# RMSNorm with ReLU on one core: one semaphore per SBUF slot that counts its loads and stores, in place of one per transfer

## The chip, the cores and the metric

The kernel runs on one core of a Trainium2 chip. The metric is device time in microseconds (us) of one execution; the times given are medians of several executions. The profile is one further look at a single execution; its span, from the first to the last instruction, is about 1.8 us shorter than the time.

## The reference

```python
# x: 16 x 1024 x 512 float32, gamma: 512 float32, eps = 1e-5
rms = np.sqrt(np.mean(x ** 2, axis=-1, keepdims=True) + eps)
return np.maximum(x / rms * gamma, 0).astype(np.float32)
```

Each of the 16384 rows is read once and written once: 33.55 MB in and 33.55 MB out, 67.11 MB in all.

## The kernel before

The rows are cut into 8 chunks of 4 MB, each 128 partitions by 16 rows of 512 numbers. SBUF has 6 slots of that size. SP issues every load and store; DVE multiplies in place; a chunk's result is stored from the slot that it was loaded into. Chunk 0 is loaded in two halves so that compute may start early. Chunks 6 and 7 use slots 0 and 1 again, and are loaded once stores 0 and 1 have landed. A "block" is half a chunk, 8 rows a partition; there are 16, and the semaphore `done` counts them.

```python
loads = [(0, 0, G), (0, G, K - G)] + [(i, 0, K) for i in range(1, nchunks)]
sem_ld = [tc.alloc_semaphore(f"ld{i}") for i in range(len(loads))]   # 9
sem_st = [tc.alloc_semaphore(f"st{i}") for i in range(nchunks)]      # 8
# ... sem_g, sem_e, sem_z, ready, sq, done, sa, sv

for m, (i, a, r) in enumerate(loads):       # SP
    if i < nslots:
        load(m)
nxt = nslots
for i in range(nchunks):
    nc.sync.wait_ge(done, per * (i + 1))
    store(i)
    if i >= 1 and nxt < nchunks:
        nc.sync.wait_ge(sem_st[nxt - nslots], 16)
        # ... load(m) of chunk nxt
        nxt += 1

for m, (i, a, r) in enumerate(loads):       # POOL tells ACT what has landed
    nc.gpsimd.wait_ge(sem_ld[m], 16)
    nc.gpsimd.sem_inc(ready, r // G)

# ... ACT: 16 blocks of squares, sums and roots; DVE: reciprocal, x * rstd * gamma, relu
#     then_inc(done, 1) on each relu

with nc.sync.register("landed") as landed:  # SP, at the end
    nc.sync.reg_mov(landed, 16)
    for i in range(nchunks):
        nc.sync.wait_ge(sem_st[i], landed)
```

## Time and profile before

| | before |
|---|---|
| time, median of the first 3 runs | 162.71 us (162.61 to 162.89) |
| span of the profiled run | 161.2 us |
| bytes moved, mean rate | 67.12 MB, 416 GB/s over the span |
| DVE, ACT busy | 126.0 us, 86.3 us |
| last landing of a store, end of the span | 160.04 us, 161.16 us |

The costliest groups of compute (line, engine, operation, tiles, shape, count; then busy us, mean ns of one; then idle time before them and what ended it) and the issues of transfers (count, size, median us from issue to landing) of the kernel before:

```profile
L115 ACT ACTIVATE junk<-slots 128x512 f32 x128 | 74.5, 582 | 30.8 <-ACTq L111 30.5
L139 DVE SCALAR_TENSOR_TENSOR slots<-slots,rstd,gamma_sb 128x512 f32 x128 | 86.2, 747 | 4.8 <-DVEq L136 4.8
...
out_dram<-slots SPq DMA_DIRECT2D x8, 4096.0 KB, 31.4
slots<-in_x_dram SPq DMA_DIRECT2D x7, 4096.0 KB, 30.4
```

ACT waits 30.5 us for data. A store takes 31.4 us from issue to landing, yet its 4 MB take only about 9.8 us of the engines at 430 GB/s (4.19 MB by the rate that the stretches of the prediction show): most of the rest it stands in the queue behind others.

### The profile page before, as it was taken

Reading aid. Unit: us, or ns where it says so; the run is one execution under the profiler, and the core shown is the slowest. Engines: PE = TensorE matmul, PEld = TensorE weight load, DVE = VectorE, ACT = ScalarE, POOL = GpSimd, SP = SyncE. Lnnn points to the kernel's source line nnn. Section 1 sums busy time; section 2 is a strip of 40 time slices with the busy share of each in tenths; the row PEclk is TensorE's granted clock in tenths of the full one; section 3 lists DMA queues with packets and bytes.
Section 4 is the critical chain, followed back from the end, with each engine's and each line's share of the span. In section 5 each row is a group of like instructions: output and inputs, shape, how many; then the busy total and the mean of one; then the engine's idle time right before and its main releaser. Section 6 shows DMA issues by size and latency. Waiting matters only on the chain. (4 is left out here: it accounts for less than half of the span.)

```text
span 161.2 us, 1006 instructions
## 1 busy us (share of the span) xinstructions
DVE 126.0 (78%) x164; ACT 86.3 (54%) x273; POOL 0.2 (0%) x4
## 2 busy tenths in 40 slices
DVE  1103989898989898999999999999999999993000
ACT  3088929889988988988900298503994000000000
POOL 0000000000000000000000000000000000000000
DMA  5999999999999999999999999999999999999993
GB/s 155 433 439 431 496 390 415 496 390 399 512 390 390 512 399 390 390 399 512 390 399 504 399 399 496 407 399 488 407 407 488 407 407 480 415 407 464 431 390 138
DMA packets 2456, 67.12 MB, mean 416 GB/s; under 512 B 276, under 2 KB 276, under 8 KB 280
## 3 DMA queue, kind: packets, MB, share of 16 engines
q1 hardware_dynamic: 2448, 67.11, 97.4%
q10 hardware_dynamic: 8, 0.01, 0.0%
HBM read 33.56 MB, written 33.55 MB: 416 GB/s over the span
## 5 line engine op out<-in xcount | busy, mean ns | idle before, releaser
L115 ACT ACTIVATE junk<-slots 128x512 f32 x128 | 74.5, 582 | 30.8 <-ACTq L111 30.5
L139 DVE SCALAR_TENSOR_TENSOR slots<-slots,rstd,gamma_sb 128x512 f32 x128 | 86.2, 747 | 4.8 <-DVEq L136 4.8
L146 DVE TENSOR_SCALAR slots<-slots x16 | 36.7, 2294 | 2.4 <-DVEq L145 0.2
L115 ACT ACTIVATION_READ_ACCUMULATOR junk<-slots x128 | 23.9, 187 | 0.0
L133 DVE RECIPROCAL rstd<-rms x16 | 3.2, 197 | 6.4 <-DVEq L129 6.4
L122 ACT ACTIVATE rms<-ss,eps_sb x16 | 4.8, 301 | 3.0 <-ACTq L121 3.0
L126 DVE LOAD_MASK_SELECT gamma_sb<-gseed x1 | 0.0, 14 | 5.8 <-DMA gseed<-in_gamma_dram 5.8
L107 ACT ACT_TABLE_LOAD x1 | 1.3, 1283 | 2.8 <-issue 2.8
L100 DVE MEMSET gseed<- 128x512 f32 x1 | 0.5, 485 | 1.1 <-SPq L81 1.1
L126 DVE STREAM_SHUFFLE gamma_sb<-gseed 128x512 f32<-128x512 f32 x1 | 0.7, 716 | 0.0
L168 POOL MEMSET const-bfloat16-1.0<- 128x1 bf16 x1 | 0.1, 102 | 0.0
L168 POOL MEMSET const-uint8-127<- 128x1 uint8 x1 | 0.1, 102 | 0.0
L168 POOL MEMSET const-float32-1.0<- 128x1 f32 x1 | 0.1, 99 | 0.0
L168 POOL MEMSET const-float32-0.0<- 128x1 f32 x1 | 0.1, 98 | 0.2 <-issue 0.2
L101 DVE MEMSET eps_sb<- 128x1 f32 x1 | 0.1, 59 | 0.0
## 6 DMA issues: line engine op xcount, KB each, us to landing
out_dram<-slots SPq DMA_DIRECT2D x8, 4096.0 KB, 31.4
slots<-in_x_dram SPq DMA_DIRECT2D x7, 4096.0 KB, 30.4
slots<-in_x_dram SPq DMA_DIRECT2D x2, 2048.0 KB, 9.7
gseed<-in_gamma_dram ACTq DMA_DIRECT2D x1, 8.0 KB
```

Of the source, the lines that this page charges most:

```text
L100: nc.vector.memset(gseed, 0.0).then_inc(sem_z, 1)
L101: nc.vector.memset(eps_sb, eps).then_inc(sem_e, 1)
L107: nc.scalar.preload_act_table(ACTF.Sqrt)
L115: a = nc.scalar.activation(out=junk[:, j, :], in_=slots[:, bass.ds(base + j * d, d)], func=ACTF.Square, accum_out=ss[:, bass.ds(col + j, 1)])
L122: nc.scalar.activation(out=rms[:, bass.ds(col, G)], in_=ss[:, bass.ds(col, G)], func=ACTF.Sqrt, bias=eps_sb, scale=inv_d).then_inc(sq, 1)
L126: nc.vector.stream_shuffle(gamma_sb, gseed, [0] * 32)
L133: nc.vector.reciprocal(out=rstd[:, bass.ds(col, G)], in_=rms[:, bass.ds(col, G)]).then_inc(sv, 1)
L139: r = nc.vector.scalar_tensor_tensor(out=row, in0=row, scalar=rstd[:, bass.ds(col + j, 1)], in1=gamma_sb, op0=ALU.mult, op1=ALU.mult)
L146: nc.vector.tensor_scalar_max(out=blk, in0=blk, scalar1=0.0).then_inc(done, 1)
L168: nc = _bacc.Bacc("TRN2", target_bir_lowering=False, num_devices=1)
```

## The change

The intent is to need fewer semaphores: 6 slot counters and one for the first half-load, where there were 9 and 8, and one for both memsets where there were two. Loads and stores of a slot alternate, so the counter goes up by 16 with each, and the thresholds follow from the turn: 16 loaded, 32 stored, 48 loaded again, 64 stored again.

```diff
@@ -54,10 +54,11 @@
 
 
     loads = [(0, 0, G), (0, G, K - G)] + [(i, 0, K) for i in range(1, nchunks)]
-    sem_ld = [tc.alloc_semaphore(f"ld{i}") for i in range(len(loads))]
-    sem_st = [tc.alloc_semaphore(f"st{i}") for i in range(nchunks)]
+
+
+    sem_half = tc.alloc_semaphore("half")
+    sem_slot = [tc.alloc_semaphore(f"slot{s}") for s in range(nslots)]
     sem_g = tc.alloc_semaphore("gam")
-    sem_e = tc.alloc_semaphore("epsr")
     sem_z = tc.alloc_semaphore("zero")
     ready = tc.alloc_semaphore("ready")
     sq = tc.alloc_semaphore("sq")
@@ -72,10 +73,18 @@
     def load(m):
         i, a, r = loads[m]
         nc.sync.dma_start(out=slot_ap(i)[:, a:a + r, :],
-                          in_=xv[i][:, a:a + r, :]).then_inc(sem_ld[m], 16)
+                          in_=xv[i][:, a:a + r, :]
+                          ).then_inc(sem_half if m == 0 else sem_slot[i % nslots], 16)
+
+    def loaded(engine, m):
+        i = loads[m][0]
+        if m == 0:
+            engine.wait_ge(sem_half, 16)
+        else:
+            engine.wait_ge(sem_slot[i % nslots], 32 * (i // nslots) + 16)
 
     def store(i):
-        nc.sync.dma_start(out=ov[i], in_=slot_ap(i)).then_inc(sem_st[i], 16)
+        nc.sync.dma_start(out=ov[i], in_=slot_ap(i)).then_inc(sem_slot[i % nslots], 16)
 
     ctx.enter_context(tc.manual_schedule(engines={mybir.EngineType.SP}))
     with tc.tile_critical():
@@ -87,25 +96,25 @@
             nc.sync.wait_ge(done, per * (i + 1))
             store(i)
             if i >= 1 and nxt < nchunks:
-                nc.sync.wait_ge(sem_st[nxt - nslots], 16)
+                nc.sync.wait_ge(sem_slot[nxt % nslots], 32)
                 for m, (c, a, r) in enumerate(loads):
                     if c == nxt:
                         load(m)
                 nxt += 1
 
         for m, (i, a, r) in enumerate(loads):
-            nc.gpsimd.wait_ge(sem_ld[m], 16)
+            loaded(nc.gpsimd, m)
             nc.gpsimd.sem_inc(ready, r // G)
 
         nc.vector.memset(gseed, 0.0).then_inc(sem_z, 1)
-        nc.vector.memset(eps_sb, eps).then_inc(sem_e, 1)
+        nc.vector.memset(eps_sb, eps).then_inc(sem_z, 1)
 
         nc.scalar.wait_ge(sem_z, 1)
         nc.scalar.dma_start(out=gseed[0:P:32, :],
                             in_=gamma[None, :].to_broadcast([P // 32, d])
                             ).then_inc(sem_g, 16)
         nc.scalar.preload_act_table(ACTF.Sqrt)
-        nc.scalar.wait_ge(sem_e, 1)
+        nc.scalar.wait_ge(sem_z, 2)
         with nc.scalar.Fori(0, ngroups) as gi:
             nc.scalar.wait_ge(ready, 1)
             nc.scalar.sem_inc(ready, -1)
@@ -146,9 +155,12 @@
             nc.vector.tensor_scalar_max(out=blk, in0=blk, scalar1=0.0).then_inc(done, 1)
 
     with nc.sync.register("landed") as landed:
-        nc.sync.reg_mov(landed, 16)
-        for i in range(nchunks):
-            nc.sync.wait_ge(sem_st[i], landed)
+        nc.sync.reg_mov(landed, 32)
+        for s in range(nchunks - nslots, nslots):
+            nc.sync.wait_ge(sem_slot[s], landed)
+        nc.sync.reg_mov(landed, 64)
+        for s in range(nchunks - nslots):
+            nc.sync.wait_ge(sem_slot[s], landed)
 
 
 # ---- launch: one core; inputs and outputs as the reference has them ----
```

## The prediction

> **What bounds the kernel now.** I read the page of the profile first: the span, the busy shares, the slices and the DMA queues.
>
> ```profile
> span 161.2 us, 1006 instructions
> ...
> DVE 126.0 (78%) x164; ACT 86.3 (54%) x273; POOL 0.2 (0%) x4
> ...
> DMA  5999999999999999999999999999999999999993
> ...
> q1 hardware_dynamic: 2448, 67.11, 97.4%
> ```
>
> The reader is to see that no compute engine is near full, and that one queue, the one that the sync engine (SP) fills with all loads and stores, keeps the 16 DMA engines at nine tenths or more in 38 of 40 slices. Next I cut the span into stretches (columns: stretch, its length, busy time of DVE, ACT and POOL with counts, granted clock, DMA share, GB/s).
>
> ```profile
> 2.00:30.00 28.00, 15.29 (x22) 18.08 (x55) 0.00 (x0) 1.00 1.01 429
> 30.00:60.00 30.00, 28.36 (x38) 27.63 (x90) 0.00 (x0) 1.00 1.00 427
> 60.00:90.00 30.00, 28.21 (x37) 19.32 (x63) 0.00 (x0) 1.00 1.01 429
> 90.00:120.00 30.00, 28.51 (x38) 18.64 (x60) 0.00 (x0) 1.00 1.00 430
> 120.00:146.00 26.00, 24.66 (x31) 2.62 (x9) 0.00 (x0) 1.00 1.00 430
> 146.00:158.00 12.00, 0.49 (x1) 0.00 (x0) 0.00 (x0) 1.00 1.01 437
> 158.00:161.20 3.20, 0.00 (x0) 0.00 (x0) 0.00 (x0) 1.00 0.03 10
> ```
>
> From 2 to 158 us the DMA share never falls below 1.00, at 427 to 437 GB/s. The 67.12 MB of the page at 430 GB/s are 156.1 us, which is this stretch. Compute ends at 146.5 us (start 144.20 plus 2.29, the last row of the timeline) and the transfers run 12 us longer. So the sum that sets the time is: about 1.5 us of start, 156 us of transfers, and a tail of about 3 us with nothing in transfer. Then I asked the waits of the DMA-issuing queue on SP (total us, times, longest us).
>
> ```profile
> SPq L78 <- DVE slots L146: 105.4, 6, 26.6
> SPq L74 <- DMA out_dram<-slots: 32.9, 2, 24.1
> SPq L151 <- DMA out_dram<-slots: 12.5, 2, 9.6
> ```
>
> SP waits 105.4 us for finished blocks and 32.9 us for two slots to come free; all of that lies beneath transfers already queued, as the full DMA share shows. Only the end of the third line (L151, the final waits for all stores) is on the path, since nothing follows the last landing but the end of the program. For that tail I read three source lines: the program's last one between 160.6 and 161.3 us, the final waits, and the register move ahead of them (count, ns least/median/most, first and last start).
>
> ```profile
> L182 POOLq EVENT_SEMAPHORE_RANGE_CLEAR  x1: 201/201/201, 160.7 to 160.7; - x1
> ...
> L151 SPq EVENT_SEMAPHORE  x4: 17/28/28, 147.4 to 160.1; - x4
> ...
> L149 SPq MOVE  x1: 43/43/43, 147.3 to 147.3; - x1
> ```
>
> The records behind them give the order: the last store's 16 increments land from 158.70 to 160.04 us, SP's last final wait is released at 160.06, all engines meet at 160.5, POOL clears the semaphores from 160.66 to 160.86, and a second meeting ends the span at 161.16. So 1.1 us lie between the last landing and the end, and semaphore instructions are all that is in it.
>
> **What the Trainium skill says.** The page DMA: Bandwidth & Descriptors, section "Why a DMA increments its semaphore by 16 and not by 1", says that each engine taking part adds one when its data has landed, and warns that two transfers in flight on one semaphore can let a wait pass early; it asks for one semaphore per in-flight slot. The trace agrees on the count: 16 landings for each load and store. In its section "Anatomy of one DMA" it says that DMA engines wait on no semaphore, the issuing sequencer does, and that the semaphore write is nearly free beside the write receipt. The trace shows the first side: load 6 was issued at 72.07 us, 16 ns after store 0's last increment at 72.06. The page Perfetto Trace Analysis, section "Per-engine timelines", says that a sequencer-only instruction's record holds its execution alone, not its wait or propagation; hence the 17 and 28 ns of the L151 rows are the cost, and the microseconds before them the wait. The page Runtime: NRT & Kernel Launch, section "The ~15µs preamble/postamble breakdown", lists a reset of 51 semaphores per engine around the kernel; [...]no run here shows it. I count nothing for it.
>
> **The change part by part.** I compared both built programs engine by engine: every engine has the same shown instructions in the same order, SP has 40 and POOL 31 in all in both programs, and the transfers are the same with the same shapes. Only which semaphore is named, and against which value, differs.
>
> 1. *Loads and stores.* Same 17 transfers on the same queue; each still adds 16. Which counter it adds to touches no byte that moves. Cost 0.
>
> 2. *The two waits before loads 6 and 7.* Before: store 0's own semaphore at 16. After: slot 0 at 32, which is the second half-load of chunk 0 plus store 0. By the landing records that half-load landed at 13.27 us and store 0 at 72.06, so 32 is reached at 72.06, exactly when the old wait was. For slot 1: load 22.98, store 81.95, so 81.95. On one slot no two transfers fly together on that counter, since each store is issued after its load landed (31.14 after 13.27, 47.62 after 22.98) and each reload after the store; the separate semaphore for the first half keeps even chunk 0 apart. Cost 0.
>
> 3. *POOL's nine waits that tell ACT what has landed.* Still nine, 17 ns each by the trace; they now wait for 16 or 48. 48 on slot 0 is complete when load 6 lands (91.49), as before. Cost 0.
>
> 4. *The two memsets on one counter.* ACT asked for the second memset at 2.79 us, after issuing gamma's transfer; that memset ended at 1.61 (1.551 plus 0.059). A wait for 2 on the shared counter is met just as long before. Cost 0.
>
> 5. *Final waits.* Before: one register move, eight waits packed into four L151 instructions and the closing branch. After: six waits, two register moves. The move to 64 carries slot 2's wait; it costs about 43 ns (the L149 row), but stores 2 to 5 have all landed by 140.62 us and SP gets there at 147.3, so it runs at about 147.5, beneath the last store's transfer. After the last landing, the old program ran a wait on two semaphores (28 ns) and then the branch; the new one runs a wait on slot 1 alone (17 ns, as the single wait in the L151 row) and then the same branch. On the path: minus 11 ns.
>
> 6. *Clearing at the end.* The built programs show it clearing 30 semaphores before and 19 after. It took 201 ns and stands between two meetings of all engines, so it is on the path. If its time is all per semaphore: 201 / 30 = 6.7 ns each, 11 fewer save 74 ns. If it is all fixed: 0. I take half, 37 ns; this is an estimate from one row, and the trace cannot choose.
>
> Sum: 0 - 11 - 37 = -48 ns, bounds about -85 and 0. On the median of 162.71 us that gives 162.66, or -0.03%.
>
> **The rivals.** (a) *The shared counter holds a transfer back.* If a load or the final wait had to wait for something later than before, a gap would open in the DMA share. Against: step 2's times, where the added term landed some 59 us before the deciding one. Even if a reload were issued some microseconds later, store 1 still stood ahead of it in the queue (load 6 was issued at 72.07 us, store 1 landed at 81.95, load 6 at 91.49), so that nothing would idle. The time would stay at 162.7. To cost 2% (3.3 us) the queue would have to run dry, for which nothing speaks. (b) *The shorter counter list saves more than I count.* The whole tail from the last landing to the end is 1.1 us; were a third of it proportional to the number of semaphores, the time would fall by about 0.25 us to 162.45. For it: clearing is the one long instruction there. Against: all else in the tail is meetings of engines, the same in both programs. (c) *The reloaded register falls onto the path.* If the second move ran after the last landing it would add 43 ns, and 162.75 would result; against it, it hangs on slot 2, whose last store lands at 101.46 us. (d) *Another draw of DMA throughput.* The transfers are 97% of the time; 0.2% more or less in their rate is 0.3 us, larger than all my terms, and the three runs of before already spread over 0.28 us (162.61 to 162.89), with a profiled run at 162.94.
>
> **Range and chances.** All rivals of substance stay between 162.45 and 162.75; the spread of runs (d) is wider than they are. I take 162.65 with 162.3 to 163.0: 0.35 us each way, the seen spread of 0.28 and a little for another chip or another hour. For 2% the time has to leave 159.5 to 166.0, and I know of no path that leads there: the lower end would need more than the whole 1.1 us tail to vanish three times over. Chances: faster 0.01, same 0.98, slower 0.01.
>
> **What would show each step right or wrong.** Right: the DMA share at 1.00 from 2 to 158 us and the same reload times (72.1 and 82.0 us, within the run's noise) for steps 1 and 2; nine POOL waits of 17 ns for 3; ACT's first work at 8.8 us for 4; one 17 ns wait after the last landing for 5; a clearing instruction between 127 and 201 ns for 6. The prediction would be wrong if a gap in the DMA share appears before a reload, if a final wait is released well after the last landing, if the clearing grows, or if the rate of the transfers changes with the counter they add to, which I have held to be impossible.

## The result, and the profile after

| | before | after |
|---|---|---|
| time, median of 6 runs each | 162.82 us (162.61 to 162.89) | 162.79 us (162.54 to 163.48) |
| span of the profiled run | 161.2 us | 160.9 us |
| last landing to end of span | 1.112 us | 1.029 us |

The ratio is 1.0005, with a 95% interval of 0.9985 to 1.0025: no difference that can be told. The page of the changed kernel, lines as in the prediction:

```profile
span 160.9 us, 1006 instructions
...
DVE 126.0 (78%) x164; ACT 86.3 (54%) x273; POOL 0.2 (0%) x4
...
DMA  5999999999999998999999999999999999999993
...
q1 hardware_dynamic: 2448, 67.11, 97.6%
```

The instruction counts, the busy times and the bytes are the same. The stretches of the changed kernel (columns as before):

```profile
2.00:30.00 28.00, 15.35 (x22) 18.17 (x55) 0.00 (x0) 1.00 1.01 428
30.00:60.00 30.00, 28.36 (x38) 27.63 (x90) 0.00 (x0) 1.00 1.01 429
60.00:90.00 30.00, 28.21 (x37) 19.23 (x62) 0.00 (x0) 1.00 1.00 427
90.00:120.00 30.00, 28.51 (x38) 18.81 (x60) 0.00 (x0) 1.00 1.00 431
120.00:146.00 26.00, 24.66 (x31) 2.45 (x9) 0.00 (x0) 1.00 0.99 429
146.00:158.00 12.00, 0.43 (x1) 0.00 (x0) 0.00 (x0) 1.00 1.01 437
```

The DMA share stays at 0.99 to 1.01, the rate at 427 to 437 GB/s: no gap opened. A stretch of 30 us would hide a gap of a few tenths of a us, but the packets show none either: between the first data and the last, an engine stood idle for 0.62 us in the mean, as against 0.79 us before. The waits of SP's queue in the changed kernel:

```profile
SPq L87 <- DVE slots L155: 105.2, 6, 26.5
SPq L75 <- DMA out_dram<-slots: 33.0, 2, 24.2
SPq L163 <- DMA out_dram<-slots: 12.4, 1, 12.4
```

The same three waits, within 0.2 us of before. The last is now one wait of 12.4 us in place of two, since the final waits are ordered by slot. By the landing records store 0 lands at 72.114 us and load 6 is issued at 72.131; store 1 at 82.035 and load 7 at 82.051. The last source lines of the changed kernel:

```profile
L194 POOLq EVENT_SEMAPHORE_RANGE_CLEAR  x1: 138/138/138, 160.5 to 160.5; - x1
...
L163 SPq EVENT_SEMAPHORE  x1: 17/17/17, 159.9 to 159.9; - x1
...
L161 SPq MOVE  x1: 29/29/29, 147.4 to 147.4; - x1
```

The clearing of 19 semaphores takes 138 ns, where 30 took 201. The wait released by the last store is a single one of 17 ns, and the second register move is made at 147.4 us, beneath the last store. The tail is 0.083 us shorter. The rest of the 0.25 us between the two spans (160.90 and 161.16 us) is transfers: the last landing came at 159.88 us in this run and at 160.04 in the other.

### The profile page after: what moved, and what is told of

Same layout as the page of the kernel before. It is cut to its first block, busy times and chain, and to the rows that moved or that the text cites. A ratio compares the mean times of both kernels' runs of the same rounds, so it can differ in the third digit from the quotient of the medians.

```text
span 160.9 us, 1006 instructions
## 1 busy us (share of the span) xinstructions
DVE 126.0 (78%) x164; ACT 86.3 (54%) x273; POOL 0.2 (0%) x4
```

## The experiments

My theory: the transfers set the time, no counter holds one of them back, and the only trace of the change is in the tail, by the number of semaphores cleared. Rivals: the shared counters delay a reload; the increments on them cost transfer time; the tail got shorter for another reason. All kernels gave the correct result. Each group of runs has its own runs of the kernel before beside it.

### The size of chance: both kernels once more

No edit: e1 is the kernel before, e2 the changed one, five rounds each.

> The kernel before against itself: the size of chance. My theory (transfers set the time, and their rate wanders by some 0.2%): ratio 1.000 with an interval of about 0.2% each way; the clearing instruction again at 201 ns. A rival that the two semaphore schemes differ by a real few tenths of a per cent would need this interval to be much narrower than the one of the changed kernel.

> The changed kernel once more, with five rounds. My theory: the tail is 0.08 us shorter, the transfers wander by more, ratio 1.000 within 0.2% either way (0.9995 if the tail alone showed); last landing to end of span 1.03 us, clearing 138 ns. Rival (the shared counters slow or delay transfers): ratio of 1.001 or more with an interval that leaves out 1.

| run | median | ratio to before, 95% interval | last landing to end |
|---|---|---|---|
| e1, before against itself | 162.99 us | 1.0007 (0.9994 to 1.0020) | 1.113 us |
| e2, changed kernel | 162.81 us | 0.9993 (0.9980 to 1.0006) | 1.029 us |

The kernel before differs from itself by as much as the changed one differs from it. The rival ratio of 1.001 or more is ruled out by the interval of e2. The tail, however, came out at 1.11 us for the one and 1.03 us for the other both times that each was profiled: a difference of 0.084 us can be read from the trace even though 0.2% of time, 0.3 us, hides it on the clock. The intervals were a little narrower than the 0.2% that I had expected.

### Does the number of semaphores make the tail?

e3 adds 11 semaphores that nothing uses, e4 adds 100:

```diff
     sv = tc.alloc_semaphore("sv")
+    spare = [tc.alloc_semaphore(f"spare{i}") for i in range(11)]   # e4: range(100)
```

> The changed kernel with 11 semaphores allocated and never used, so that 30 are cleared as before, while loads and stores still share the slot counters. My theory (each cleared semaphore costs 5.7 ns, from 201 and 138 ns for 30 and 19): clearing back at 201 ns, last landing to end about 1.09 us, time not told apart from before. Rival (the clearing got shorter for another reason, such as which semaphores stood nonzero or when it started): clearing stays near 138 ns.

> The changed kernel with 100 unused semaphores more, 119 cleared. My theory: clearing takes 29 + 119 x 5.7 = 707 ns, 570 more than in the changed kernel, all on the path: last landing to end about 1.60 us, time about 163.3 us, ratio 1.003. Rival (the cost of clearing is in steps or mostly fixed): clearing under 300 ns, ratio 1.000.

The clearing instruction of e3:

```profile
L195 POOLq EVENT_SEMAPHORE_RANGE_CLEAR  x1: 201/201/201, 160.5 to 160.5; - x1
```

The clearing instruction of e4:

```profile
L195 POOLq DRAIN  x2: 34/131/228, 160.5 to 161.5; - x2
...
L195 POOLq EVENT_SEMAPHORE_RANGE_CLEAR  x1: 680/680/680, 160.8 to 160.8; - x1
```

| semaphores cleared | kernel | clearing | last landing to end | median | ratio to before |
|---|---|---|---|---|---|
| 19 | changed (e2) | 138 ns | 1.029 us | 162.81 us | 0.9993 (0.9980 to 1.0006) |
| 30 | e3 | 201 ns | 1.101 us | 162.78 us | 1.0003 (0.9991 to 1.0014) |
| 30 | before (e1) | 201 ns | 1.113 us | 162.99 us | 1.0007 (0.9994 to 1.0020) |
| 119 | e4 | 680 ns | 1.710 us | 163.43 us | 1.0033 (1.0020 to 1.0046) |

With 30 semaphores the clearing is back at 201 ns to the nanosecond, though the transfers still share their counters: its length goes by the count of semaphores, not by what they count. From 19 to 119 the clearing grows by 542 ns, 5.4 ns each, and the tail by 0.68 us, 6.8 ns each. The tail grows by more than the clearing because the drain on POOL just ahead of it is longer too (88 ns in the changed kernel, 99 ns before and in e3, 228 ns in e4): 542 and 140 ns make the 0.68 us. Why the drain grows is left open. These are means over 11 and 100 semaphores, and a single one need not show: e9 and e10 below clear 20, in 139 ns behind a drain of 83 ns, and their tail is 1.029 us, as with 19. So e4's time was foreseen (163.3 us, measured 163.43), its clearing was 27 ns shorter and its tail 0.11 us longer than foreseen. e3's tail is 12 ns shorter than that of the kernel before with the same 30 semaphores: that is the final wait on one semaphore in place of two, 11 ns by their records.

### What does a met wait cost on the path?

e5 puts the wait for the last store first, so the others come after it.

```diff
+        nc.sync.reg_mov(landed, 64)
+        for s in reversed(range(nchunks - nslots)):
+            nc.sync.wait_ge(sem_slot[s], landed)
         nc.sync.reg_mov(landed, 32)
         for s in range(nchunks - nslots, nslots):
             nc.sync.wait_ge(sem_slot[s], landed)
-        nc.sync.reg_mov(landed, 64)
-        for s in range(nchunks - nslots):
-            nc.sync.wait_ge(sem_slot[s], landed)
```

> The changed kernel with the wait for the last store put first, so that the register move back to 32 and the waits for slots 4, 5, 3 and 2, all met long before, come after the last landing. My theory: a met wait costs 53 to 67 ns from start to start (the spacing of such instructions in the trace), so two instructions more on the path and the move make about 0.13 us: release of the last wait to the closing branch about 0.18 us, in place of 0.057, last landing to end about 1.16 us, the time the same within noise. Rival (waits that are already met cost nothing): tail stays at 1.03 us. Rival (waits against registers are slow): tail longer by 0.5 us or more.

The final waits of e5, from 140 us on:

```profile
L161 SPq MOVE  x1: 29/29/29, 160.1 to 160.1; - x1
...
L163 SPq EVENT_SEMAPHORE  x2: 17/22/27, 160.1 to 160.2; - x2
```

All three now start after the last landing at 160.059 us: at 160.075, 160.139 and 160.192, and the closing branch at 160.260. Here the move carries the wait for the last store. From release to branch are 0.185 us, where the changed kernel has 0.057. The tail is 1.156 us, as foreseen (1.16), and the time is not told apart from before: 162.92 us, ratio 0.9994 (0.9955 to 1.0032; one run of before at 163.87 us widens the interval). A met wait thus costs 53 to 68 ns on the path, far more than the 17 to 28 ns of its record, and register waits are not otherwise slow.

### How much delay could a counter have caused for free?

The prediction held that a reload may come some microseconds later at no cost. Four runs put one more wait before both reloads of the changed kernel, for an event that comes later. In e6 that event is the relu of block 8, in e7 the landing of store 1, in e9 the seventh of eight multiplications of block 8, in e10 the first half of the relu of block 8. It is load 6 that the wait holds back; load 7 is issued at 81.8 to 82.7 us in all four, as against 82.05 in the changed kernel.

```diff
                 nc.sync.wait_ge(sem_slot[nxt % nslots], 32)
+                nc.sync.wait_ge(done, 8)            # e6
+                nc.sync.wait_ge(sem_slot[1], 32)    # e7
+                nc.sync.wait_ge(mid, 8)             # e9, e10: mid is a new semaphore
...
+                if j == G - 2:                      # e9, on the multiplications
+                    r.then_inc(mid, 1)
...
-            nc.vector.tensor_scalar_max(out=blk, in0=blk, scalar1=0.0).then_inc(done, 1)
+            nc.vector.tensor_scalar_max(out=lo, in0=lo, scalar1=0.0).then_inc(mid, 1)   # e10: lo, hi are the halves of blk
+            nc.vector.tensor_scalar_max(out=hi, in0=hi, scalar1=0.0).then_inc(done, 1)  # e10
```

> The changed kernel with both reloads held until eight blocks are done, some 80.6 us, in place of 72.1 us for load 6: the delay that a coarser counter could have caused, 8.5 us. My theory: store 1 keeps the engines busy until about 81.5 us, so nothing idles, the order in the queue is as before, time 162.8, same. Rival (a reload's issue time goes straight into the time): about 8 us longer.

> The changed kernel with load 6 held until store 1, the last transfer in the queue, has landed (82.0 us; 1.5 us later than in the run with eight blocks). My theory: the queue runs dry; from the last data of store 1 (some 81.4 us) to the first data of load 6 (82.05 plus 1.0 us from issue to first data, as at the start of the span) 1.6 to 2.0 us pass with nothing in transfer, and the time grows by that, to 164.4 to 164.8 us, ratio 1.010 to 1.012. Rival (later slack takes the gap up): the same time.

> The changed kernel with both reloads held until DVE has multiplied the seventh of eight rows of block 8, at about 77.5 us: load 6 comes 5.4 us later than in the changed kernel, but still some 3 us before the queue's last data (81.0 to 81.4 us). The run with 80.7 us lost 2.1 us, which my prediction had ruled out. My theory now: a delay is free only while the reload's first data (0.97 us after issue, as that run shows) can come before the engines have drained what is queued, so before an issue at about 79.8 us; here no gap and no slow packets at the reload, time 162.8, ratio 1.000. Rival (a late reload costs in proportion, some 2.1 us for 8.6 us of delay): 1.3 us longer, ratio 1.008.

> As the run before, but held until half of the last relu of block 8, at 79.5 to 80.0 us (the relu is split in two, which lengthens DVE's work by under 0.2 us a block, beneath the transfers): close to the edge. My theory: first data due at 80.5 to 81.0 us, when the first engines drain; no or next to no idle time, and at most a part of the 2.1 us. Rival (proportional): 1.8 us longer, ratio 1.011. If it is as slow as the run at 80.7 us, the edge lies earlier than the first data says[...].

e10 changes two things at once, the relu and the hold. So e11 has the split relu alone:

```diff
-            nc.vector.tensor_scalar_max(out=blk, in0=blk, scalar1=0.0).then_inc(done, 1)
+            nc.vector.tensor_scalar_max(out=lo, in0=lo, scalar1=0.0)
+            nc.vector.tensor_scalar_max(out=hi, in0=hi, scalar1=0.0).then_inc(done, 1)
```

> The control of the run before: the relu split in two as there, but the reloads held by nothing more than in the changed kernel (72.1 us). That run came out 3.0 us longer than before, more than the one held to 80.7 us. If the hold did it: DVE about 1.1 us more busy, reload at some 72.2 us, time 162.8, ratio 1.000. If the split relu did it (later stores, another rhythm of blocks): up to 1.017.

In the table, "packets" is the sum of the recorded times of the data packets, divided by 16 engines, and "idle" what is left of the time from the first data to the last.

| run | load 6 issued | median | ratio to before, 95% interval | packets | idle |
|---|---|---|---|---|---|
| changed kernel | 72.13 us | 162.79 us | 1.0005 (0.9985 to 1.0025) | 156.81 us | 0.62 us |
| e11 (control) | 72.15 us | 163.00 us | 0.9994 (0.9961 to 1.0026) | 156.99 us | 0.72 us |
| e9 | 77.44 us | 162.74 us | 0.9998 (0.9984 to 1.0011) | 156.83 us | 0.63 us |
| e10 | 80.06 us | 165.81 us | 1.0174 (1.0153 to 1.0195) | 158.67 us | 2.28 us |
| e6 | 80.72 us | 164.89 us | 1.0121 (1.0081 to 1.0160) | 158.44 us | 1.29 us |
| e7 | 81.80 us | 166.16 us | 1.0194 (1.0151 to 1.0238) | 158.68 us | 2.22 us |

By the rule of 2% all of these count as the same, but for e7, whose interval makes it unclear; e6, e7 and e10 are nonetheless longer by more than chance. The stretch from 80 to 96 us (columns as before), in the changed kernel:

```profile
80.00:96.00 16.00, 15.11 (x21) 4.84 (x16) 0.00 (x0) 1.00 1.02 438
```

in e9:

```profile
80.00:96.00 16.00, 15.11 (x21) 4.93 (x17) 0.00 (x0) 1.00 1.00 432
```

in the control e11:

```profile
80.00:96.00 16.00, 15.11 (x22) 4.54 (x16) 0.00 (x0) 1.00 1.01 430
```

in e6:

```profile
80.00:96.00 16.00, 15.11 (x21) 2.57 (x9) 0.00 (x0) 1.00 0.95 369
```

in e10:

```profile
80.00:96.00 16.00, 15.11 (x22) 1.18 (x4) 0.00 (x0) 1.00 0.97 373
```

and in e7:

```profile
80.00:96.00 16.00, 15.11 (x21) 1.47 (x5) 0.00 (x0) 1.00 0.90 340
```

The last figure is the rate. In e9 and e11 it is whole or nearly so (432 and 430 GB/s); in e6, e10 and e7 it falls to 369, 373 and 340 GB/s, and DVE's work in the stretch is the same 15.11 us in all. So a delay of 5.3 us is free, as I expected of e9, and the proportional rival (ratio 1.008) falls. But e6, which I expected at 162.8 us, lost 2.1 us, e7 lost more than the 164.4 to 164.8 us that I gave it, and e10, which I expected to lose a part of e6's loss at most, lost 3.0 us. e11 shows that the hold did this and not the split relu.

The hold keeps back more than load 6. SP issues in order, and store 2 comes after load 6: at 72.51 us in the changed kernel, at 77.83 in e9, 80.45 in e10, 81.10 in e6 and 82.19 in e7, though the last relu of its chunk had ended by 64.5 us in all of them. So the queue ran out because a blocked SP held a finished store as well as the reload. Whether a late reload alone would cost anything, with store 2 issued ahead of the wait, was not tested.

What the packets show: store 1's last data ended between 80.7 and 81.5 us on the several engines in these runs (the increments that follow it show it). In e6 the first data of load 6 came at 81.69, 0.97 us after the issue, so the engines stood idle for a moment; and the first packets after it took 1.2 to 2.1 us where most 32 KB packets take 1.213. In e6 the last packets of load 6, just ahead of store 2 (about 91 us), took 2.0 to 2.2 us once more, and in e7 some there took up to 2.3 us, where the changed kernel has 1.21 to 1.25; e10 has up to 2.5 us there. Packets like these are not found at a restart alone: in every kernel here, with no restart, those at 58 to 61 us, where the loads give way to store 0, take up to 1.8 to 2.2 us (2.03 in the changed kernel). In e7 the idle time grew by 2.22 - 0.62 = 1.60 us, as foreseen (1.6 to 2.0); the other 158.68 - 156.81 = 1.87 us, slower packets, were not. In e10 the first packets of load 6 came one after another, from 81.23 to 83.00 us, though it was issued 0.66 us earlier than in e6. With the 0.97 us of e6 its data would have come at 81.03 us, when the first engine ended store 1 at 81.02 and the last at 81.54. So the edge lies earlier than the issue-to-data time says, somewhere between an issue at 77.44 and one at 80.06 us. Why the packets are slow stays open. That e10 is worse than e6 is not quite shown: their intervals touch, and they ran on different chips (7 and 15).

### Do the increments themselves cost time?

e8 issues every transfer as two, of the even and of the odd partitions, each adding 16 to the same counter; thresholds double.

```diff
-        nc.sync.dma_start(out=slot_ap(i)[:, a:a + r, :],
-                          in_=xv[i][:, a:a + r, :]
-                          ).then_inc(sem_half if m == 0 else sem_slot[i % nslots], 16)
+        for h in range(2):
+            nc.sync.dma_start(out=slot_ap(i)[h:P:2, a:a + r, :],
+                              in_=xv[i][h:P:2, a:a + r, :]
+                              ).then_inc(sem_half if m == 0 else sem_slot[i % nslots], 16)
 # ... the store likewise; every threshold on these counters doubled
```

> The changed kernel with each transfer issued as two, of the even and of the odd partitions, so that the data packets stay 32 KB and the engines the same, while the increments of the shared counters double, from 17 x 16 to 34 x 16, with two transfers in flight on one counter (waits are for the full sum). My theory (an increment costs its engine the 9 ns of its record): 17 more on each engine, 0.15 us, time 162.8 to 163.2, same. Rival (increments of a shared counter stall the transfers): 1 us or more longer.

The time was 163.39 us, ratio 1.0024 (0.9985 to 1.0063): neither my upper end of 163.2 nor the rival's 1 us or more. The increments are records of 4 bytes that take 9 ns each; their sum per engine went from 0.153 to 0.306 us, the 0.15 us that I counted. Yet in the profiled run they don't show: the last data ended 0.76 us later than in the changed kernel, of which 0.34 us is a later first data (2.29 us in place of 1.96; the first issue of SP's queue took 563 ns in place of 387) and 0.52 us is longer data packets, most of it at 55 to 65 us, where in every kernel here the long run of loads gives way to store 0; the idle time, in which the increments lie, fell by 0.10 us. The slow packets may come from the division as such, so e8 doesn't measure the cost of the increments alone. Doubling them and dividing the transfers together cost 0.55 us by the medians, and the interval reaches up to 1.0 us, the lower end of what the rival said, so that this run doesn't quite exclude it. The change itself leaves the number of increments as it was, and for it e2 decides.

## Why the prediction was right

The prediction of 162.65 us (162.3 to 163.0, the same within 2% at 0.98) stands beside 162.79 us. It starts from a sum of 1.5 us of start, 156 of transfers and about 3 with nothing in transfer. The last of these was misread: the stretches book a packet where it starts, and by the ends of the packets the data moved from 1.95 to 159.56 us, so that only 1.60 us follow. Nothing in the prediction's terms rests on it. By its steps:

1. *Loads and stores cost nothing more.* Right: rates of 427 to 437 GB/s in both, and e2's ratio of 0.9993.
2. *The two reload waits are met at the same moment.* Right: load 6 followed store 0's last increment by 17 ns, load 7 store 1's by 16 ns.
3. *POOL's nine waits.* Right: nine waits of 17 ns in the trace after.
4. *The two memsets on one counter.* Right: ACT's first square starts at 8.72 us, as against 8.78 before, because the first load landed 0.06 us earlier.
5. *Final waits, minus 11 ns.* Right: one wait of 17 ns for one of 28, and 12 ns between e3 and e1. The register move, put at about 43 ns, was 29 ns and lies at 147.4 us, off the path. But the 17 and 28 ns of the records are not what a wait costs, as the prediction took them: the branch starts 57 ns after the one wait and 68 ns after the other (e5 has the like). The difference is 11 ns either way.
6. *The clearing.* The mechanism was right and the size was off: it was given half of 74 ns, 37, because one row could not tell a fixed cost from one by count. It is nearly all by count: 63 ns less in the clearing, and e3 and e4 put 6.5 to 6.8 ns of tail on each semaphore, so 11 fewer make about 72 to 75 ns. Of this, 11 ns lie in POOL's drain (88 ns, as against 99), which the prediction did not see: it held that all else in the tail was the same in both programs.

The sum was -48 ns with bounds of -85 and 0. The tail shows -83 ns: -11 for the wait, -63 for the clearing and -11 for the drain, with 2 ns elsewhere the other way. That it comes so near the bound of -85 is luck, since the bound has no drain in it and took all of the clearing to go by count. None of it can be seen in the time, since the same kernel differs from itself by 0.07% (0.1 us) in e1: rival (d), another draw of the transfers, is larger than what the change did, as the prediction said. Rival (a), a counter that holds a transfer back, did not happen; but the argument against it, that with a reload some microseconds later nothing would idle, holds for 5.3 us (e9) and fails at 7.9 us and more (e10, e6, e7), with store 2 held as well. The loss of 2%, 3.3 us, for which "the queue would have to run dry", was nearly reached by e7 (1.94%), where it did; so that rival deserved a working-out of where the queue ends. Rival (b) is what e4 makes of it: more semaphores, more tail, but 0.25 us would take 37 of them. Rival (c) did not happen; e5, which puts a move and two waits on the path, lost 0.13 us in the tail, and from the start of the move to that of the next instruction were 64 ns, not 43. For a gain of 2% the tail would have to vanish 2.9 times over (3.2 of 1.1 us), not over three times as written.

## What to carry to other kernels

Here the transfers queued deeply, and regrouping the semaphores that count them changed no time that could be told, since each wait still ended with the same transfer. Check this in your kernel by asking which increment was the last that the old wait and the new one needed. A delay stops being free before the queue runs empty: here an issue 3.4 us before the first engine was through with what stood in the queue was free (e9), one 1.0 us before was not (e10). And ask what else the waiting engine has yet to issue: here a finished store stood behind the wait. What a semaphore cost here was its clearing at the end, with the drain ahead of it, and, if its wait came after the last landing, the wait itself: count those before you look for more.

## What the Trainium skill lacked or had wrong

- No page has the clearing of semaphores that a kernel's own program ends with. The runs show 138, 201 and 680 ns for 19, 30 and 119 semaphores, and in the mean over 11 and 100 more of them 6.5 to 6.8 ns of time to the end for each, used or only allocated.
- The page Perfetto Trace Analysis says that wait and propagation are not in a sequencer instruction's record, but not how much of a wait that is already met the record leaves out. Here it was 53 to 68 ns from start to start, with 17 to 27 ns recorded (e5).
- The page DMA: Bandwidth & Descriptors, section "Rules for kernel authors", advises to issue early, and not how early. An issue at 77.44 us was free and one at 80.06 us cost 3.0 us, with engines that drained between 80.7 and 81.5 (store 2 was held too). No page tells that 32 KB packets take up to 2.0 us in place of 1.213 where loads give way to stores, as at 58 to 61 us in the changed kernel, and up to 2.5 us after a restart (e10).
